# Two hidden pairs of every feed-forward layer multiplied without the seven-product scheme, and the stream sums made earlier

## The chip, the cores and the metric

The kernel runs on one core of one Trainium2 chip. The metric is the device time in microseconds (us) of one execution; a profile of one execution is taken beside it. The engines are named as in the profile: PE is TensorE (matmuls), PEld its weight loads, DVE VectorE, ACT ScalarE, POOL GpSimd, SP SyncE. The last two issue most of the DMAs here.

## What is computed

One step of a trunk of two layers for 512 frames of a prompt and 32 frames of a sample stream, together T = 544 columns, model width 1024, hidden width 2816, all in fp32:

```
for i in range(DEPTH):
    x = x + FFN_RES * swiglu(rms_norm(x, p['ffn1_norm'][i]), ...)
    ...                                   # conv module for i = 0, differential attention for i = 1
    x = x + m
    x = x + FFN_RES * swiglu(rms_norm(x, p['ffn2_norm'][i]), ...)
y = rms_norm(x, p['final_norm'])

def swiglu(h, w_gate, w_up, w_down):
    return (jax.nn.silu(h @ w_gate) * (h @ w_up)) @ w_down
```

So there are four feed-forward layers, called FFN0 to FFN3 here, in the order FFN0, conv mixer, FFN1, FFN2, attention mixer, FFN3, final norm. The caches and states that the mixers return don't bear on the change.

## The kernel before

**Data.** The stream x lies transposed in eight tiles x0 to x7 of 128 channels by 544 columns. A product in fp32 is three matmuls in a rounded format (high x high, high x low, low x high): each operand is split into a high part (`whi`, `xh`, `hh`), made by ACT, and a low part (`wlo`, `xl`, `hl`), made by DVE as the difference. A matmul takes 128 x 128 weights and 272 of the 544 columns.

**A feed-forward layer.** Hidden channels are done in 22 blocks of 128, each with a gate and an up row. Rather than multiply gate and up with both halves of the columns and all eight tiles (2 x 8 x 2 x 3 = 96 matmuls), a block uses a scheme of seven products P1 to P7 over quarters of the matrices (7 x 4 x 3 = 84 matmuls). The scheme needs differences of the stream (`xd`, L395, `quarters`), sums of the stream (`xt`, split to `xth` and `xtl`, L415, `quarter_sums`), and sums of the weights: `ws`, to which POOL adds by an accumulating DMA (`add_stripe`, L268), and `s`, made by DVE (`total`, L606). The normalisation factor r of a column is multiplied in behind the products: squares of x are summed over channels by small matmuls with a matrix of ones (L463), then come a root on ACT, a reciprocal on DVE and a spread to all partitions by two DMAs over DRAM (`norm_c`, L494). FFN0 and FFN2 give each tile's squares to PE (`square`, `add_squares`, L443); FFN1 and FFN3 add them up on DVE in `acc` first (`norm_sq`, L372). The down products (D) are done in groups of blocks (`FCH`, L33), with x updated after each (`evict`, L628).

**Order.** `layer_order` (L152) writes the order of the products (jobs) by hand. `task` puts the work of DVE and ACT at a job's number; on each engine it runs in the order written. FFN0 starts P1 0, P1 1, P2 0, P2 1, P1 2, P2 2, P5 0, ... . FFN1 and FFN2 are one program; there FFN2's first products stand between the last eight down products of FFN1. The stream sums are made after the last x of a layer is known, except for FFN2, where they stand at the down products 4 to 7. Weights come through rings of tiles (`wr`, `ws`, `wd`) by SP's queue; a ring's next load is issued when its oldest tile was used.

**Memory.** PSUM has a pool for the feed-forward layers, with tiles pq (2, of two banks), pd (1, of two banks) and py (2, of one bank), and one for each mixer (tiles a; m and t). A pool is closed before the next one opens, and the next pool's first instruction waits for all tiles of the old one. X's and Z's sums of the scheme share a pq tile, each a bank of it.

## Time and profile before

| what | us |
|---|---|
| median of three runs | 2069.58 |
| lowest and highest of them | 2066.18, 2071.45 |
| the profiled execution | 2068.29 |
| its span in the trace | 2066.5 |
| TensorE busy in it | 1969.7 |
| VectorE busy | 1537.5 |
| ScalarE busy | 1001.9 |

The trace belongs to the profiled execution, which lies between the lowest and the median run. The span runs from the first instruction to the last; the 1.8 us that the execution is longer lie around it. Busy times are sums over instructions: an engine that is busy 95% of the span can still be at its limit in one stage and wait in another, so the stages are looked at one by one below.

### The profile page before, as it was taken

What the parts mean: (1) busy time and instruction counts of PE and PEld (TensorE: products, weight loads), DVE (VectorE), ACT (ScalarE), POOL (GpSimd) and SP (SyncE); (2) the same over time, 40 slices, a digit from 0 to 9 for tenths busy, and PEclk for the clock granted to TensorE, in tenths of its full rate; (3) what the DMA queues carried; (4) which work ended last, traced back from release to release, by engine and by line L of the source; (5) the groups of instructions that cost most, each with busy time, mean ns of one, the idle gap of its engine ahead of it and who ended that gap; (6) DMA issues with size and microseconds to landing.
All of it is one profiled execution on the core that took longest, in us unless ns stands there. A gap on an engine that the chain in (4) does not pass through costs nothing.

```text
span 2066.5 us, 39057 instructions
## 1 busy us (share of the span) xinstructions
PE 1969.7 (95%) x15564; PEld 1923.2 (93%) x15564; DVE 1537.5 (74%) x2748; ACT 1001.9 (48%) x1931; POOL 184.0 (9%) x217
## 2 busy tenths in 40 slices
...
GB/s 190 176 157 147 139 142 94 77 126 171 145 62 196 151 155 143 144 142 156 23 192 153 146 152 139 97 93 84 89 84 89 63 126 192 158 142 145 144 73 74
DMA packets 114405, 267.01 MB, mean 129 GB/s; under 512 B 12040, under 2 KB 27952, under 8 KB 114224
## 3 DMA queue, kind: packets, MB, share of 16 engines
...
q8 instruction: 123, 2.02, 0.4%
...
HBM read 255.16 MB, written 9.31 MB: 128 GB/s over the span
## 4 chain that ended last, share of the span: by engine, by line
PE 80%; DVE 8%; ACT 5%; DMA 4%; issue 1%; SPq 0%; POOL 0%; DVEq 0%; ACTq 0%; POOLq 0%
PE pq L527 34%; PE pd L345 7%; PE pd L351 7%; PE pd L348 7%; PE py L527 5%; DMA ws<-gu 2%; PE a L345 2%; PE a L348 2%; PE a L351 2%; PE m L345 2%; DVE wlo L119 2%; PE m L348 2%; PE m L351 2%; PE a L843 1%; ACT whi L302 1%
## 5 line engine op out<-in xcount | busy, mean ns | idle before, releaser
L527 PE MATMUL pq<-xh,whi 128*128 128x272 f32 x1008 | 296.3, 294 | 27.0 <-ACT whi L1440 7.6
L527 PE MATMUL pq<-xh,wlo 128*128 128x272 f32 x1008 | 294.6, 292 | 2.6 <-DVE wlo L119 2.6
L527 PE MATMUL pq<-xth,whi 128*128 128x272 f32 x1008 | 290.6, 288 | 4.5 <-DVE u L119 4.5
L527 PE MATMUL pq<-xl,whi 128*128 128x272 f32 x1008 | 292.7, 290 | 0.4 <-DVE xl L410 0.2
L527 PE MATMUL pq<-xtl,whi 128*128 128x272 f32 x1008 | 290.0, 288 | 0.0
L527 PE MATMUL pq<-xth,wlo 128*128 128x272 f32 x1008 | 289.3, 287 | 0.0
L119 DVE TENSOR_TENSOR wlo<-wr,whi 128x512 fp32r<-128x512 f32 (+1 forms) x228 | 186.7, 823 | 123.6 <-ACT whi L302 122.6
L345 PE MATMUL pd<-hh,whi 128*128 128x272 f32 x1272 | 264.9, 290 | 3.6 <-DVE x L635 3.6
L348 PE MATMUL pd<-hl,whi 128*128 128x272 f32 x1272 | 262.5, 287 | 0.0
L351 PE MATMUL pd<-hh,wlo 128*128 128x272 f32 x1272 | 262.4, 288 | 0.0
L302 ACT ACTIVATE whi<-wd 128x512 fp32r<-128x512 f32 (+1 forms) x280 | 166.5, 600 | 145.6 <-issue 117.1
L527 PEld LDWEIGHTS pq<-xh,whi 128*128 128x128 f32 x1008 | 192.7, 191 | 32.8 <-ACT whi L1440 8.2
L272 POOL DMA_DIRECT2D ws<-gu x88 | 106.0, 1211 | 1303.5 <-DVE wlo L119 919.3
L119 DVE TENSOR_TENSOR wlo<-wd,whi 128x512 fp32r<-128x512 f32 (+1 forms) x280 | 183.2, 655 | 36.7 <-ACT whi L302 33.0
L345 PEld LDWEIGHTS pd<-hh,whi 128*128 128x128 f32 x1272 | 199.0, 188 | 4.6 <-issue 4.6
L348 PEld LDWEIGHTS pd<-hl,whi 128*128 128x128 f32 x1272 | 200.1, 189 | 0.0
L351 PEld LDWEIGHTS pd<-hh,wlo 128*128 128x128 f32 x1272 | 199.1, 188 | 0.0
L119 DVE TENSOR_TENSOR wlo<-ws,whi 128x512 fp32r<-128x512 f32 x176 | 120.4, 687 | 101.7 <-ACT whi L302 101.6
L527 PEld LDWEIGHTS pq<-xh,wlo 128*128 128x128 f32 x1008 | 192.9, 191 | 3.2 <-DVE wlo L119 3.1
L527 PEld LDWEIGHTS pq<-xth,whi 128*128 128x128 f32 x1008 | 189.6, 188 | 6.4 <-ACT e L569 2.6
L527 PEld LDWEIGHTS pq<-xl,whi 128*128 128x128 f32 x1008 | 192.8, 191 | 0.9 <-DVE xl L410 0.9
L527 PEld LDWEIGHTS pq<-xth,wlo 128*128 128x128 f32 x1008 | 190.0, 188 | 0.0
...
## 6 DMA issues: line engine op xcount, KB each, us to landing
...
wd<-dn SPq DMA_DIRECT2D x128, 256.0 KB, 2.9
...
```

The lines of the kernel that those rows point to most:

```text
L119: nc.vector.tensor_tensor(out=out, in0=in0, in1=in1, op=op)
L272: nc.gpsimd.dma_start(out=c["t"].rearrange("p (a c) -> p a c", a=2), in_=c["add"], accum_op=ALU.add)
L302: nc.scalar.activation(out=hi, in_=src, func=AF.Copy)
L345: nc.tensor.matmul(out=ps[:, s, :HT], lhsT=wh, rhs=xh[:, s * HT:(s + 1) * HT], start=first, stop=False)
L348: nc.tensor.matmul(out=ps[:, s, :HT], lhsT=wh, rhs=xl[:, s * HT:(s + 1) * HT], start=False, stop=False)
L351: nc.tensor.matmul(out=ps[:, s, :HT], lhsT=wl, rhs=xh[:, s * HT:(s + 1) * HT], start=False, stop=last)
L527: nc.tensor.matmul(out=out, lhsT=wt[:, a:a + P], rhs=b, start=first and k == 0 and z == 0, stop=last and k == 3 and z == 2, skip_group_che ...
L843: nc.tensor.matmul(out=o, lhsT=w[:, t * P:(t + 1) * P], rhs=xt[:, q, t:t + NU], start=t == 0, stop=t == NJ - 1)
```

## The change

- Blocks 0 and 1 of each layer (`PLAIN = 2`) are multiplied plainly. Their jobs are Ga, Gb (gate with tiles 0 to 3 and 4 to 7) and Ua, Ub (up), 24 matmuls each; r is multiplied in from PSUM (`by_r`). They stand first in each layer, so the scheme starts with block 2. In FFN2, Ga 0 stands between the down products 5 and 6 of FFN1, the other plain jobs behind the last.
- The stream sums of FFN1 and FFN3 for k = 0 to 2 are made in the mixer's last outputs (o = 4 to 6), the fourth early in the layer. Those of FFN0 and FFN2 are made at jobs around Ga 1. The low half of one set is made where the next set starts. The differences are made behind the plain jobs (`quarter_diff`), over the second half of `xh` and `xl`.
- All layers sum their squares on DVE (`norm_sq`). The weights of the scheme's first blocks are loaded behind the spread of r.
- PSUM: pq becomes four single banks; X and Z have one each. Last down products use pairs of single banks ("qq", "yy") and are evicted in two operations.
- Pools are opened with `reuse_waits="tile"`: the first use of a new tile waits for the old tiles that lay there, not for the whole pool. One pool `ar` of six tiles serves the conv weights, the sums of the stream and attention's splits.
- In the conv mixer and in attention, the norm's matmuls move some steps back; attention's first q step isn't taken before step 14.
- The prologue loads and splits gate and up of block 0 instead of the gates of blocks 0 and 1. `FCH` becomes (2, 4, 4, 4, 4, 4).

The diff, cut to its core:

```diff
-FCH = (3, 4, 4, 4, 3, 4)
+FCH = (2, 4, 4, 4, 4, 4)
 QC = 512
 AHEAD = 4
+PLAIN = 2
...
+        head = "Ga 0 Ua 0 Gb 0 Ub 0 Ga 1 Ua 1 Gb 1 P1 2 Ub 1 P2 2 P1 3 P2 3 P6 2 P6 3 P5 2 P7 2 P7 3 P5 3 P4 2".split()
+        head = list(zip(head[::2], map(int, head[1::2])))
         if f:
-            order += held[:4]
-            for d, (kind, i) in zip(held[4:], (("P1", 0), ("P1", 1), ("P5", 0), ("P5", 1))):
-                go(kind, i)
-                order.append(d)
-            head = "P2 0 P2 1 P1 2 P2 2 P5 2"
-        else:
-            head = "P1 0 P1 1 P2 0 P2 1 P1 2 P2 2 P5 0 P5 1 P5 2"
-        head = (head + " P6 0 P6 1 P6 2 P7 0 P7 1 P4 0 P3 0 P7 2 P4 1 P3 1 P4 2 P1 3 P3 2 P2 3").split()
-        for kind, i in zip(head[::2], head[1::2]):
-            go(kind, int(i))
...
+            order += held[:6]
+            go(*head.pop(0))
+            order += held[6:]
+        for kind, i in head:
+            go(kind, i)
+        down = [("D", f, o, 0) for o in range(KD)]
+        for i in range(PLAIN + 1, KF):
+            first = i == PLAIN + 1
+            if not first:
+                go("P6", i)
+            go("P3", i - 1)
...
+                if kind in ("Ga", "Ua"):
+                    (gate if kind == "Ga" else both)[f, i] = chunk("wr", g[2 * i + (kind == "Ua")], DM, 2)
...
+    def quarter_diff(k, gc):
+
+        todo = nst.pop("diff", None)
         if k < KD // 2:
...
+            d = ffn_pool[0].tile([P, HT], F32, tag="e", name="xd", bufs=8)
+            two(d, x[k][:, :HT], x[k][:, HT:], ALU.subtract)
+            nst["diff"] = (d, xh[k][:, HT:], xl[k][:, HT:], vcol(gc + k))
...
+        if k == 0:
+            nst["t"] = [arena() for _ in range(6)]
+        todo = nst.pop("sum", ())
+        if k < KD // 2:
+            b = tp.tile([P, T], F32, tag="g", name="xg")
+            nc.scalar.activation(out=b, in_=x[k + KD // 2], func=AF.Copy, scale=vcol(gc + k + KD // 2))
+        for src, h, l in todo:
+            nc.scalar.activation(out=h, in_=src, func=AF.Copy)
+        if k < KD // 2:
...
-            nc.vector.scalar_tensor_tensor(out=t4, in0=t[:, HT:], scalar=-1.0, in1=b[:, :HT],
+            nc.vector.scalar_tensor_tensor(out=b[:, :HT], in0=t[:, HT:], scalar=-1.0, in1=b[:, :HT],
...
-        with tc.tile_pool(name="hp", bufs=1) as hp, \
-             tc.tile_pool(name="pf", bufs=1, space=bass.MemoryType.PSUM) as pf:
+        with tc.tile_pool(name="hp", reuse_waits="tile", bufs=1) as hp, \
+             tc.tile_pool(name="pf", reuse_waits="tile", bufs=1, space=bass.MemoryType.PSUM) as pf:
...
+            def by_r(tag, kind):
+
+                if "sum" in nst:
+                    quarter_sums(KD // 2, None)
+                t = b[tag] = tp.tile([P, T], F32, tag=tag, name=tag)
+                ps = st[kind, f, m]
+                if isinstance(ps, list):
+                    for z, p in enumerate(ps):
+                        two(t[:, z * HT:(z + 1) * HT], p[:, :HT], nst["r"][:, z * HT:(z + 1) * HT], ALU.mult)
+                else:
+                    two(halves(t), pv(ps), halves(nst["r"]), ALU.mult)
...
+            if m < PLAIN:
+                g1 = at["Ga", f, 1, c] + (2 if f == 0 and entry else 1)
+                n1 = max(at["Gb", f, m, c] + 1, g1)
+                n2 = max(at["Ub", f, m, c] + 1, g1)
+                task(n1, lambda: by_r("g", "G"))
+                task(n1, silu)
+                task(n2, lambda: by_r("u", "U"))
+                task(n2, prod, True)
+                n3 = n2 + (3 if m else 1)
+                task(n3, hidden)
+                task(n3, hidden_lo, True)
+                return
...
-            nc.vector.scalar_tensor_tensor(out=halves(x[o]), in0=pv(ps), scalar=0.5, in1=halves(x[o]),
-                                           op0=ALU.mult, op1=ALU.add)
+            for out, src in [(x[o][:, z * HT:(z + 1) * HT], p[:, :HT]) for z, p in enumerate(ps)] \
+                    if isinstance(ps, list) else [(halves(x[o]), pv(ps))]:
+                nc.vector.scalar_tensor_tensor(out=out, in0=src, scalar=0.5, in1=out, op0=ALU.mult, op1=ALU.add)
...
+            for ring, n in DEPTH.items():
+                while nload[ring] < n:
+                    load(ring)
...
-        if entry == "start":
-            for k in range(KD):
-                task(2 + k, lambda k=k: square(k))
-        else:
-            task(8, norm)
-        for k in range(KD // 2):
-            task(k, lambda k=k: quarter_sums(k, which[0][0]), True)
+        for f in range(len(which)):
+            g1 = at["Ga", f, 1, 0]
+            start = entry and f == 0
+            task(g1 - (1 if f else 0 if start else 2), norm)
+            gc = which[f][0]
+            sums_at = (-1, 0, 1, 4, 5) if start else (-2, -1, 0, 4, 5) if f else (None, None, None, -3, -2)
+            for k, n in enumerate(sums_at):
+                if n is not None:
+                    task(g1 + n, lambda gc=gc, k=k: quarter_sums(k, gc), True)
+            for k in range(KD // 2 + 1):
+                task(g1 + 3 + k, lambda gc=gc, k=k: quarter_diff(k, gc), True)
...
-                held = j["c"] == len(FCH) - 1 and (i < KD // 2 or f + 1 == len(which))
-                ps = st["d", f, i, j["c"]] = ptile("q" if i % 2 and held or (j["c"], i) == (len(FCH) - 2, KD - 1) else "d")
+                tag = "d"
+                if j["c"] == len(FCH) - 1:
+                    tag = ("d", "qq", "d", "qq", "yy", "d" if f + 1 < len(which) else "qq", "yy", "d")[i]
+                elif (j["c"], i) == (len(FCH) - 2, KD - 1):
+                    tag = "qq"
+                ps = st["d", f, i, j["c"]] = ptile(tag)
                 for k in range(j["n"]):
                     hh, hl = hid[f, j["m0"] + k]
                     mm3(ps, (hi[:, off:], lo[:, off:]), k, hh, hl, k == 0, k == j["n"] - 1)
             else:
-                if kind == "P1":
-                    st["q", f, i] = ptile("d" if i == 2 else "q")
+                if kind in ("Ga", "Ua"):
+                    st[kind[0], f, i] = ptile({("Ga", 1): "yy", ("Ua", 1): "d"}.get((kind, i), "qq"))
+                elif kind == "P1":
+                    st["x", f, i] = ptile("q")
+                elif kind == "P5":
...
+                if kind[0] in "GU":
+                    for k in range(4):
+                        kk = k + 4 * (kind[1] == "b")
+                        mm3(st[kind[0], f, i], (hi[:, off:], lo[:, off:]), k, xh[kk], xl[kk], kk == 0, kk == KD - 1)
+                    u["left"] -= 1
+                    continue
...
             if first:
-                proj(pg, w_get(), range(KD - 2))
-                norm_a(alloc()[:, 0, :], [nst["acc"]], AF.Sigmoid)
-                proj(pg, cur[0], range(KD - 2, KD))
+                proj(pg, w_get())
                 pa = alloc()
                 proj(pa, w_get(), range(1))
+                norm_a(alloc()[:, 0, :], [nst["acc"]], AF.Sigmoid)
+                proj(pa, cur[0], range(1, KD - 2))
                 norm_b(alloc())
...
             norm_sq(o)
+            if o < KD - 1:
+                quarter_sums(o - KD // 2, next_gc)
...
-                at_step(24 * h + 8 * i + 8 + c["f"][i], f, h)
+                at_step(max(24 * h + 8 * i + 8 + c["f"][i], 14), f, h)
...
+                norm_sq(k)
             for c in gates:
                 used(c)
                 used(c)
+            load("ws")
...
         def between(o):
             quarters(o, V_F1 + KD)
-            square(o)
-            if o >= KD // 2:
-                quarter_sums(o - KD // 2, V_F1 + KD)
+            norm_sq(o)
...
-        with tc.tile_pool(name="psa", bufs=4, space=bass.MemoryType.PSUM) as pp:
+        with tc.tile_pool(name="psa", reuse_waits="tile", bufs=4, space=bass.MemoryType.PSUM) as pp:
             conv(psum(4, [P, 2, 512], pp, "a", 4), V_F2)
...
-
-        with tc.tile_pool(name="psb", bufs=2, space=bass.MemoryType.PSUM) as pp:
+            if KD // 2 <= o < KD - 1:
+                quarter_sums(o - KD // 2, V_F2 + KD)
+
+        with tc.tile_pool(name="psb", reuse_waits="tile", bufs=2, space=bass.MemoryType.PSUM) as pp:
             attn(psum(2, [P, 2, 512], pp, "m", 2), psum(4, [P, 512], pp, "t", 4), into_ffn)
```

How the order of instructions moves is shown at three places. Names carry the number of a buffer; a row is line, operation, output <- inputs, shape.

DVE in the conv mixer's tail, before: from the eviction of x6 (L987) past that of x7. `acc` adds a square, `xl` is a low part for FFN1, `wlo` the low part of FFN1's weights, `xt` the first stream sum.

```order
L987 SCALAR_TENSOR_TENSOR x6_93<-a_6820,vecs_72,x6_93 128x544
L410 SCALAR_TENSOR_TENSOR xl5_6814<-x5_92,vecs_72,xh5_6813 128x544
L119 TENSOR_TENSOR acc_6658<-acc_6658,sq_6880 128x544
L119 TENSOR_TENSOR wlo_6885<-wr_6622,whi_6884 128x512
L119 TENSOR_TENSOR wlo_6885<-wr_6698,whi_6884 128x512
L987 SCALAR_TENSOR_TENSOR x7_94<-a_6883,vecs_72,x7_94 128x544
L410 SCALAR_TENSOR_TENSOR xl6_6877<-x6_93,vecs_72,xh6_6876 128x544
L119 TENSOR_TENSOR acc_6658<-acc_6658,sq_6943 128x544
L410 SCALAR_TENSOR_TENSOR xl7_6940<-x7_94,vecs_72,xh7_6939 128x544
L119 TENSOR_TENSOR wlo_6973<-wr_6762,whi_6972 128x512 x2
```

The same place after the change, from the eviction of x6 to that of x7 (L1030); `xt` and the write to `xg` are a set of sums for k = 2, `ar` the low halves of the set for k = 1:

```order
L1030 SCALAR_TENSOR_TENSOR x6_94<-a_6801,vecs_75,x6_94 128x544
L405 SCALAR_TENSOR_TENSOR xl5_6785<-x5_93,vecs_75,xh5_6784 128x544
L123 TENSOR_TENSOR acc_6630<-acc_6630,sq_6861 128x544
L435 SCALAR_TENSOR_TENSOR xt_6868<-x2_90,ngain_87,xg_6864 128x272
L437 SCALAR_TENSOR_TENSOR xt_6868<-x2_90,ngain_87,xt_6868 128x272
L439 SCALAR_TENSOR_TENSOR xg_6864<-xt_6868,xg_6864 128x272
L123 TENSOR_TENSOR ar_6719<-xt_6795,ar_6716 128x544
L123 TENSOR_TENSOR ar_6721<-xg_6791,ar_6718 128x272
L123 TENSOR_TENSOR wlo_6876<-wr_6597,whi_6875 128x512
L123 TENSOR_TENSOR wlo_6876<-wr_6658,whi_6875 128x512
L1030 SCALAR_TENSOR_TENSOR x7_95<-a_6874,vecs_75,x7_95 128x544
```

Between the two evictions stand five operations for the stream sums that stood behind the last eviction before.

DVE at the down products between FFN1 and FFN2, before: from the eviction of x5 (L635) to that of x6, with a set of stream sums in between (`xt`, `xt4`, `xtl`):

```order
L635 SCALAR_TENSOR_TENSOR x5_92<-pd_11496,x5_92 128x544
L410 SCALAR_TENSOR_TENSOR xl5_11531<-x5_92,vecs_72,xh5_11530 128x544
L427 SCALAR_TENSOR_TENSOR xt_11537<-x1_88,ngain_86,xg_11535 128x272
L429 SCALAR_TENSOR_TENSOR xt_11537<-x1_88,ngain_86,xt_11537 128x272
L431 SCALAR_TENSOR_TENSOR xt4_11538<-xt_11537,xg_11535 128x272
L119 TENSOR_TENSOR xtl1_11540<-xt_11537,xth1_11539 128x544
L119 TENSOR_TENSOR xtl1_11540<-xt4_11538,xth1_11539 128x272
L119 TENSOR_TENSOR wlo_11526<-wr_10884,whi_11525 128x512
L119 TENSOR_TENSOR wlo_11593<-wr_11030,whi_11592 128x512
L635 SCALAR_TENSOR_TENSOR x6_93<-pd_11563,x6_93 128x544
```

After, from the eviction of x2 (L658) past that of x3, which comes in two halves:

```order
L658 SCALAR_TENSOR_TENSOR x2_90<-pd_11278,x2_90 128x544
L123 TENSOR_TENSOR acc_11236<-acc_11236,sq_11311 128x544
L405 SCALAR_TENSOR_TENSOR xl2_11309<-x2_90,vecs_75,xh2_11308 128x544
L123 TENSOR_TENSOR wlo_11342<-wd_11130,whi_11341 128x512
L658 SCALAR_TENSOR_TENSOR x3_91<-pq_11314,x3_91 128x272
L658 SCALAR_TENSOR_TENSOR x3_91<-pq_11315,x3_91 128x272
L123 TENSOR_TENSOR acc_11236<-acc_11236,sq_11352 128x544
L405 SCALAR_TENSOR_TENSOR xl3_11350<-x3_91,vecs_75,xh3_11349 128x544
L123 TENSOR_TENSOR wlo_11342<-wr_10848,whi_11341 128x512
```

The sums are gone from here; each tile's square is now added to `acc` on DVE, and the add stands ahead of the tile's low part.

SP's queue at FFN0's start, before, up to the spread of r (`row`, then `r`):

```order
L262 DMA wd_159<-gu0 128x512
L262 DMA wd_161<-gu0 128x512
L262 DMA wd_163<-dn0 128x384
L262 DMA ws_468<-gu0 128x1024
L262 DMA ws_490<-gu0 128x1024
L262 DMA wr_509<-gu0 128x1024
L262 DMA wd_517<-dn0 128x384
L491 DMA row_540<-r4_535 4x136
L492 DMA r_539<-row_540 128x544
```

After:

```order
L268 DMA wr_143<-gu0 128x1024
L1468 DMA vecs_75<-vec 128x317
L268 DMA wr_214<-gu0 128x1024
L268 DMA wr_216<-gu0 128x1024
L268 DMA ws_218<-gu0 128x1024
L479 DMA row_352<-r4_347 4x136
L480 DMA r_351<-row_352 128x544
L268 DMA ws_355<-gu0 128x1024
L268 DMA ws_357<-gu0 128x1024
```

The spread of r has moved ahead of the loads of `ws` for the later blocks and of `wd`, which now follow it.

## Rows read from the trace of the kernel before

**Rows 1.** The page, part 1 (busy us, share of the span, instructions) for TensorE, and part 4, the chain that ended last, by engine.

```profile
PE 1969.7 (95%) x15564; PEld 1923.2 (93%) x15564; DVE 1537.5 (74%) x2748; ACT 1001.9 (48%) x1931; POOL 184.0 (9%) x217
...
PE 80%; DVE 8%; ACT 5%; DMA 4%; issue 1%; SPq 0%; POOL 0%; DVEq 0%; ACTq 0%; POOLq 0%
```

**Rows 2.** Busy time by stretch, the whole program: for each stretch in us from the span's start its length, then busy us and instructions of TensorE, its weight loads, DVE, ACT and POOL, the granted clock of TensorE as a share of 2.4 GHz, the share of the DMA engines, GB/s. The first is the start of FFN0, the second steady work, then the starts of FFN1, FFN2 and FFN3.

```profile
0.00:80.00 80.00, 55.66 (x389) 48.70 (x390) 57.98 (x120) 46.60 (x91) 10.52 (x18) 0.89 0.68 186
80.00:360.00 280.00, 280.00 (x2240) 280.00 (x2239) 208.19 (x366) 133.75 (x261) 18.07 (x15) 1.00 0.52 140
...
620.00:680.00 60.00, 48.33 (x353) 45.92 (x352) 48.29 (x88) 35.25 (x67) 8.47 (x7) 0.94 0.71 184
...
960.00:1065.00 105.00, 93.61 (x738) 87.82 (x737) 80.50 (x144) 58.22 (x109) 6.05 (x5) 0.98 0.42 112
...
1670.00:1728.00 58.00, 47.46 (x345) 45.00 (x345) 46.79 (x86) 34.14 (x65) 8.44 (x7) 0.94 0.70 185
```

**Rows 3.** The waits of TensorE over the whole span: tile and line that waited, who was waited for, us in total, times, longest.

```profile
PE py L463 <- DVE e L119: 8.8, 1, 8.8
PE pq L527 <- ACT whi L1440: 7.6, 3, 5.3
...
PE pq L527 <- ACT whi L302: 6.8, 2, 3.4
...
PE m L345 <- DVE x L635: 3.6, 1, 3.6
PE a L345 <- DVE x L635: 3.6, 1, 3.6
PE pd L345 <- DVE x L635: 3.6, 4, 1.4
```

**Rows 4.** TensorE at FFN0's start and FFN2's: the group of the small squares' matmuls in the stretch 0 to 80 and in 960 to 1065 (busy us, mean ns | idle before), and between them two rows of the timeline (start, us): the last of the first 48 products, and what came next.

```profile
L463 PE MATMUL py<-sq,ones_d 128*32 128x136 f32 x64 | 4.2, 345 | 8.8 <-DVE e L119 8.8
...
19.01 0.29 PE L527 MATMUL py<-xh,wlo 128*128 128x272 f32 x1
28.14 0.68 PE L463 MATMUL py<-sq,ones_d 128*32 128x136 f32 x8 [8.83 <-DVE e L119]
...
L463 PE MATMUL py<-sq,ones_d 128*32 128x136 f32 x64 | 3.6, 298 | 0.0
```

**Rows 5.** DVE at the end of the conv mixer and the start of FFN1, from the timeline (start, us, engine, line, operation, tiles; in brackets its idle time before and who ended it): one output of the mixer up to the next one's eviction (L987), then one set of stream sums and its low halves; the last row is an output of the attention mixer.

```profile
612.24 0.78 DVE L987 SCALAR_TENSOR_TENSOR x<-a,vecs,x 128x544 f32<-128x544 f32 x1
...
614.39 0.72 DVE L119 TENSOR_TENSOR acc<-acc,sq 128x544 f32<-128x544 f32 x1 [0.68 <-ACT sq L378]
...
616.24 0.78 DVE L987 SCALAR_TENSOR_TENSOR x<-a,vecs,x 128x544 f32<-128x544 f32 x1
...
626.57 0.50 DVE L427 SCALAR_TENSOR_TENSOR xt<-x,ngain,xg 128x272 f32<-128x272 f32 x1
...
628.34 1.08 DVE L119 TENSOR_TENSOR xtl<-xt,xth 128x544 fp32r<-128x544 f32 x2 [0.25 <-ACT xth L434]
629.33 0.49 DVE L427 SCALAR_TENSOR_TENSOR xt<-x,ngain,xg 128x272 f32<-128x272 f32 x1
...
1672.42 0.72 DVE L1334 TENSOR_TENSOR x<-m,x 128x544 f32<-128x544 f32 x1 [2.01 <-PE m L351]
```

**Rows 6.** FFN1's last down products before FFN2, from the timeline: the eviction of x4 on DVE, then on ACT the high part and the square of it.

```profile
999.89 0.72 DVE L635 SCALAR_TENSOR_TENSOR x<-pd,x 128x544 f32<-128x544 f32 x1
...
1000.64 0.75 ACT L406 ACTIVATE xh<-x,vecs 128x544 fp32r<-128x544 f32 x1 [1.39 <-DVE x L635]
1001.30 0.64 ACT L445 ACTIVATE sq<-x 128x544 f32<-128x544 f32 x1
```

**Rows 7.** The spread of r, from the timeline: SyncE's DMAs (`SPq`: the row to DRAM, then from there to 128 partitions) and the first use on DVE in FFN0, and the two DMAs in FFN1.

```profile
51.47 0.60 SPq L491 DMA_DIRECT2D row<-r  x1
56.18 0.33 SPq L492 DMA_DIRECT2D r<-row  x1
...
61.67 0.44 DVE L119 TENSOR_TENSOR g<-e,r 128x272 f32<-128x272 f32 x1 [1.33 <-DMA r<-row]
...
647.68 0.52 SPq L491 DMA_DIRECT2D row<-r  x1
649.28 0.33 SPq L492 DMA_DIRECT2D r<-row  x1
```

**Rows 8.** The entry of the conv mixer, from the timeline: the evictions of x5 and x7 (L635) on DVE, then TensorE's last matmul of FFN0 and its first of the mixer.

```profile
401.28 0.72 DVE L635 SCALAR_TENSOR_TENSOR x<-pq,x 128x544 f32<-128x544 f32 x1
...
407.03 0.72 DVE L635 SCALAR_TENSOR_TENSOR x<-pq,x 128x544 f32<-128x544 f32 x1
...
403.84 0.41 PE L351 MATMUL pq<-hh,wlo 128*128 128x272 f32 x2
407.89 0.49 PE L345 MATMUL a<-xh,whi 128*128 128x272 f32 x2 [3.65 <-DVE x L635]
```

**Rows 9.** Busy time by stretch again, short ones around the idle times of TensorE (columns as in rows 2).

```profile
28.75:40.75 12.00, 9.50 (x53) 8.11 (x50) 10.16 (x20) 7.34 (x15) 0.00 (x0) 0.50 0.11 20
...
409.50:412.50 3.00, 3.00 (x16) 3.00 (x15) 1.71 (x2) 1.81 (x2) 0.00 (x0) 0.50 0.15 22
...
1690.50:1695.00 4.50, 4.50 (x21) 4.50 (x21) 2.82 (x6) 2.21 (x5) 0.00 (x0) 0.50 0.02 4
...
1004.00:1022.00 18.00, 12.34 (x106) 10.80 (x105) 13.95 (x25) 10.31 (x20) 0.00 (x0) 1.00 0.04 12
```

215 lines of the change are left out of this document (92 added, 123 removed).

## The prediction

> **What bounds the kernel now.** I read the page's busy shares and its chain first: TensorE (PE) is busy 1969.7 of 2066.5 us and carries 80% of the chain, VectorE (DVE) 8% [rows 1]. So time is won only where PE waits or where it has fewer columns to stream. Next I read busy time stretch by stretch [rows 2]. From 80 to 360 us PE is busy all the time: 2240 matmuls in 280.00 us, 0.125 us for each 128x272 product. I call **loss** of a stretch its length less 0.125 us times its 128x272 matmuls; small norm matmuls (128x136) count as loss. The four starts of a feed-forward layer (FFN0 to FFN3) are then:
> FFN0, 0 to 80: 389 matmuls less 64 small ones [rows 4], 325 x 0.125 = 40.6, loss 39.4.
> FFN1, 620 to 680: 353 less 8 small (its one norm, where the 64 were eight), 345 x 0.125 = 43.1, loss 16.9.
> FFN2, 960 to 1065: 738 less 64 small [rows 4], 674 x 0.125 = 84.2, loss 20.8.
> FFN3, 1670 to 1728: 345 less 8, 337 x 0.125 = 42.1, loss 15.9.
> Together 93.0 us, the stock the change can draw on. The waits of PE [rows 3] say what they are made of: 8.8 us behind `e` at the first squares, 7.6 and 6.8 us for weight halves (`whi`), and, at the entry of either mixer, 3.6 us for the last eviction of x.
>
> **The added matmuls.** A plain block takes 96 products of 128x272 where the seven-product form takes 84. Two blocks in each of four layers: 8 x 12 = 96 more, x 0.125 = **+12.0 us**, all on PE and on the path, since PE has no idle time in the steady part [rows 2].
>
> **FFN0's start.** PE finished its first 48 products at 19.3 us, bound by x and the weight pieces as they came, and then stood from 19.3 to 28.14, because the bank for the squares is freed by `e` on DVE, which stood behind two sets of stream sums there [rows 4]. In the changed order 8 plain half blocks of 24 matmuls stand there, which need x and weights alone. The same arrivals put 72 matmuls (Ga 0, Ua 0, Gb 0) at about 20 us, loss 20 - 9 = 11, and the next 100 run without the sums, to about 32.5. Behind that I expect 0 to 3 us at P1 2, whose bank is freed only when r is there: the reciprocal can be done at about 25 (my estimate: x7's square added by 20.5, then norm, root and reciprocal), and the spread of r over the partitions took 10.2 us from its first transfer's issue to its first use in this stage (51.47 to 61.67) and less elsewhere [rows 7]; I take 2. In SyncE's (SP's) queue fewer weight loads stand ahead of the row than now, and the loads for the weight sums stand behind the spread (the order excerpt), so the second of those sums may be late; that is in the next figure. Between nothing and two sets of sums (5.5 us, worked out in the next part) in the P6 and P5 products, which come quicker than DVE can make sums and weight sums: I take 5, near the upper end, since DVE has the evictions of the plain blocks to do as well. With 3 us of smaller waits and 1 of half clock (both estimates): 11 + 2 + 5 + 3 + 1 = 22. Gain 39.4 - 22 = **17.5** (16 to 19.5).
>
> **FFN1's start.** The stream sums of k = 0 to 2 move into the last three outputs of the conv mixer. There DVE needs 4.0 us for an output (612.24 to 616.24, with 0.68 us of waiting for ACT's square inside), and PE 48 x 0.125 = 6.0. A set of sums is three operations and two lows: 626.57 to 628.34 and 628.34 to 629.33, 2.8 us [rows 5]. So DVE's turn becomes 4.0 + 2.8 = 6.8, or about 6.5 if the wait inside the set is filled: it falls 0.5 to 0.8 us behind for each output and starts from a backlog here. By the end x7's eviction, which now follows PE's last product at once, comes about 3.7 us after it; Ga 0's second matmul waits for that eviction, since its bank lies under the mixer's last accumulator. With 1.5 us of half clock after it and 1 of small waits the loss is about 6. What falls away is the wait for sums and for `whi` behind them. Gain 16.9 - 6 = **10.9** (8 to 13).
>
> **FFN3's start.** The same, but in the attention mixer's tail DVE waits 2.01 us for PE before each output [rows 5], so the added 2.8 leaves it about 0.8 behind for each of three: x7 some 2.4 us late, loss 4.4. Gain **11.5** (9 to 13).
>
> **FFN2's start.** Here the sums leave the down products and the squares leave PE: DVE adds them up instead (64 small matmuls took 3.6 us [rows 4]). But the add waits for ACT, and it is written ahead of the low half: eviction 0.72, of x, then ACT's `xh` and `sq`, which end at 1001.94, 2.05 us after the eviction's start [rows 6], add 0.65, low 0.7, a weight low 0.6: 4.0, with small waits 4.5, against 24 x 0.125 = 3.0 on PE. Over eight outputs the plain Gb 0, which needs x7, ends some 6.3 us later than PE alone would (8 x 1.5 = 12 us of DVE's lag, less about 6 that the plain Ga 0 and the first part of Gb 0 fill); with up to two sets of sums, 5.5 us, waited for at P6, the loss is 6.3 to 11.8 and I take 10.8. Gain **10** (8 to 13). The excerpt of DVE's order shows the new place of the add.
>
> **The mixers' entries.** PE stood from 404.1 to 407.89 until x7 was evicted, since the pool closes as a whole [rows 8]; 3.0 us after that ran at a granted clock of 0.50, 1.2 GHz, with 16 records in place of 24 [rows 9]. With a wait for each tile the first accumulator needs x5's bank alone, evicted at 401.28 [rows 8]; x7's low half is due at k = 7, 42 matmuls or 5.2 us later, when it is there. Gain 3.65 + 1.0, less 0.1: **4.5** (2 to 6). At the attention's entry the same 3.6 us [rows 3] and up to 2 us of half clock, less about 0.8 for the q step that is moved behind: **5** (3 to 6). Removed constants, single banks of their own for X and Z, one conv tile more, and shorter first hidden chunks: nothing, PE's full stretches hide them; if that cover went, the evictions that now come in two pieces would cost at most a second 0.72 [rows 6] each, some 5 in a layer, 14 us in all.
>
> **Sum.** 17.5 + 10.9 + 11.5 + 10 + 4.5 + 5 = 59.4, less 12.0: 47.4 us. From the profiled execution's 2068.3 us (span 2066.5 and 1.8 around it; the median of the runs, 2069.6, is 1.3 above) this gives 2020.9. I predict **2021**. The ends of the terms, 46 and 70.5, less 12, give 2010 to 2034.
>
> **Rivals.**
> 1. *VectorE becomes the bound of the starts.* For: it is the engine the starts wait for already [rows 3], and each added operation is in order behind a wait for ACT [rows 5, 6]. If a down product's turn is 5.5 us instead of 4.5 (8 us), x7 comes 3 us later in FFN1 and FFN3 (6 us), and half clock follows three times at 1.6 (5 us), the time is 2021 + 19 = **2040**. Against: most of the sums now lie beside plain products.
> 2. *r comes late everywhere.* The plain accumulators are held until r. In FFN1 the row's issue and r's were 1.6 us apart (647.68, 649.28), in FFN0 4.7 [rows 7]. With FFN0's 10.2 us in every layer, P1 2 waits 1.5 us in three layers and 3 in FFN0 instead of 2, with a little half clock: **2028**.
> 3. *The waits by tile do nothing at the mixers* (another buffer still holds the first product back): 9.5 back, **2030**.
> 4. *The starts are almost free*: three of them lose 4 us each less than I take, and 2 us of half clock are gone: **2007**. For: the sums are off PE's path in all of them. Against: the down products' 4.5 us a piece before FFN2, which nothing shortens.
> 5. *Slower: half clock through the plain heads.* In the stretch 28.75 to 40.75 PE was busy 9.50 of 12 us and yet ran at 0.50 all along [rows 9]. If the short waits for banks keep it there, a matmul takes 4.5 / 21 = 0.214 instead of 0.125 [rows 9], 2.1 us more for a half of 24; 32 halves cost 69 us, and the time is **2090**. From 22 halves on, two thirds of the heads, the change is slower than before. Against: from 1004 to 1022 PE was busy only 12.34 of 18 us, in pieces with waits of 1.4 us for banks between them, and the granted clock was 1.00, 2.4 GHz [rows 9]; the long slow stretches followed idle times of 3.4 us and more [rows 3, 8, 9], and such ones I expect at one or two places only.
> The Trainium skill speaks for this rival: "TensorE: Matmul & The Clock Gate", section "A second HAM failure mode: psum-queue depth-cycling", reports a kernel in which cycling through PSUM banks left PE idle for short times so often that its clock swung between the two levels. By that rule the time would be rival 5's. The trace agrees with it before 41 us and not from 1004 to 1022.
>
> **How the numbers follow.** About 0.3% (6 us) is what a measurement of this kernel can tell from no change. Forecast (2010 to 2034, likeliest 2021) 0.52; rival 1, 0.18; rival 2, 0.08; rival 3, 0.06; rival 4, 0.08; rival 5, 0.05; the remaining 0.03 for two of the losses together, which would end near no change. Rival 1 may reach 2045 where its lateness grows with each output. The range that leaves out no more than 2 in 10 is **2005 to 2043**: it holds the forecast, rivals 2 to 4 and most of rival 1. Faster by over 0.3%: 0.91; within 0.3%: 0.04; slower: 0.05.
>
> **What would show it.** In the changed profile: no wait of PE near 19 us and none for `e` at squares; at the mixers' entries no 3.6 us wait and a clock of 1.00; a wait of 2 to 4 us for x in FFN1's second matmul, with half clock after it; the down products before FFN2's plain head 4.5 us apart with PE waiting for x; FFN0's first 336 matmuls done at 62 to 65 us; 96 more matmuls in the full stretches at 0.125. Wrong would be: full stretches with waits (then the new banks or the shorter chunks cost something), a granted clock of 0.50 through the plain halves, or starts whose loss stays above 81 of the 93 us, from which the added products eat the gain.

## The result, and the profile after

The changed kernel takes 2019.3 us (median, 2017.7 to 2021.9) where the kernel before takes 2068.7 in the same session: ratio 0.976, 95% interval 0.9745 to 0.9780, faster by 49 us. The prediction was 2021 us, in a range of 2005 to 2043. The profiled execution took 2020.5 us, with a span of 2018.7 against 2066.5. Each kernel's time below is the median of its fast executions; one execution of both_orders took 6031.8 us and is left out.

The page of the changed kernel, busy us (share of the span) and instructions, and the chain that ended last:

```profile
PE 1964.4 (97%) x15548; PEld 1929.4 (96%) x15548; DVE 1513.4 (75%) x2722; ACT 979.2 (49%) x1873; POOL 173.9 (9%) x209
...
PE 61%; DVE 6%; ACT 4%; issue 1%; DMA 1%; POOL 0%; DVEq 0%; ACTq 0%
```

PE is busy 1964.4 us where it was 1969.7 [rows 1], though it has 96 products more: most of the small squares are gone (64 took 3.6 us in FFN2 [rows 4]), and less of it runs at half clock. The chain's shares add up to 73% only, so I read nothing from the fall of PE's from 80%. Busy time by stretch (length, busy us of PE, its weight loads, DVE, ACT and POOL, granted clock, DMA share, GB/s), the starts of FFN0, FFN1, FFN2 and FFN3 and two steady stretches between:

```profile
0.00:80.00 80.00, 67.48 (x466) 64.66 (x467) 62.56 (x126) 47.18 (x89) 8.09 (x17) 0.96 0.66 190
80.00:340.00 260.00, 260.00 (x2079) 259.88 (x2078) 196.52 (x344) 125.49 (x245) 18.55 (x17) 1.00 0.53 142
600.00:660.00 60.00, 57.27 (x457) 56.37 (x456) 44.99 (x84) 32.31 (x62) 6.05 (x5) 1.00 0.61 173
660.00:940.00 280.00, 280.00 (x2239) 279.86 (x2238) 210.60 (x370) 134.20 (x261) 21.44 (x18) 1.00 0.57 151
940.00:1045.00 105.00, 99.14 (x764) 97.63 (x763) 80.26 (x149) 56.56 (x104) 3.57 (x3) 0.97 0.33 93
1630.60:1688.60 58.00, 55.10 (x439) 54.15 (x439) 42.61 (x80) 31.87 (x61) 6.03 (x5) 1.00 0.64 178
```

Worked as in the prediction (length less 0.125 us for each 128x272 product; each start has 8 small ones now), the losses are: FFN0 80 - 458 x 0.125 = 22.75 (39.4 before), FFN1 60 - 449 x 0.125 = 3.9 (16.9), FFN2 105 - 756 x 0.125 = 10.5 (20.8), FFN3 58 - 431 x 0.125 = 4.1 (15.9) [rows 2, 4]. The steady stretches are full, so the new banks and the shorter chunks cost nothing there. The first products of the conv mixer, FFN1, the attention mixer and FFN3 (timeline of PE):

```profile
390.06 0.41 PE L352 MATMUL a<-xh,whi 128*128 128x272 f32 x2
...
602.52 0.29 PE L352 MATMUL pq<-xh,whi 128*128 128x272 f32 x1
...
1351.24 0.41 PE L352 MATMUL m<-xh,whi 128*128 128x272 f32 x2
...
1633.92 0.29 PE L352 MATMUL pq<-xh,whi 128*128 128x272 f32 x1
```

The conv mixer took 212.46 us (214.92 before, 407.89 to 622.81) and attention 282.68 (281.78, 1391.51 to 1673.29). With the 3.65 us of waiting that no longer stand ahead of each, they are 6.1 and 2.75 us shorter; but the lengths before end with a wait of FFN1's and FFN3's first product for x (0.97 and 0.91 us), which lies in the stretches of FFN1 and FFN3 too. Counted once, there, it leaves 5.1 and 1.8 for the mixers. All together:

| term | predicted gain | measured |
|---|---|---|
| FFN0's start | 17.5 | 39.4 - 22.75 = 16.6 |
| FFN1's start | 10.9 | 13.0 |
| FFN3's start | 11.5 | 11.8 |
| FFN2's start | 10 | 10.3 |
| conv mixer's entry | 4.5 | 5.1 |
| attention's entry | 5 | 1.8 |
| added products | -12.0 | -12.0 |
| sum | 47.4 | 46.6 (difference of the spans 47.8; the rest lies outside these stretches) |

What PE still waits for (tile and line that waited, who was waited for, us in total, times, longest):

```profile
PE pq L519 <- ACT e L574: 9.2, 4, 3.3
PE a L451 <- POOL d L908: 5.8, 3, 4.8
PE pq L352 <- ACT whi L1477: 5.2, 1, 5.2
...
PE pq L519 <- DVE g L123: 1.9, 1, 1.9
...
PE pq L352 <- DVE x L1030: 1.6, 1, 1.6
PE pq L352 <- DVE x L1384: 1.5, 1, 1.5
PE pq L355 <- DVE xl L405: 1.5, 1, 1.5
PE pq L352 <- ACT xh L404: 1.3, 2, 0.9
...
PE py L519 <- DVE g L123: 0.9, 1, 0.9
...
PE a L886 <- DMA ar<-wtp: 0.7, 1, 0.7
```

The 8.8 us behind `e` at the first squares and the two 3.6 us at the mixers [rows 3] are gone, and of the waits for `whi` the 5.2 us ahead of the very first product are left. What stands first now is `e` again, at another place: P6 3 is added up in the bank that holds P1 3, and ACT has to copy P1 3 into `e` before; PE waits for that copy in all four layers (3.30, 1.17, 3.30 and 1.40 us). Inside the conv mixer the wait for a weight fell from 3.5 to 0.7 us while that for POOL's `d` rose from 3.0 to 5.8; wt_five below shows that the sixth tile is not the cause.

### The profile page after: what moved, and what is told of

The parts are those of the page before. It is cut to its first block, busy times and chain, and to the rows that moved or that the text cites. A ratio compares the mean times of both kernels' runs of the same rounds, so it can differ in the third digit from the quotient of the medians.

```text
span 2018.7 us, 38721 instructions
## 1 busy us (share of the span) xinstructions
PE 1964.4 (97%) x15548; PEld 1929.4 (96%) x15548; DVE 1513.4 (75%) x2722; ACT 979.2 (49%) x1873; POOL 173.9 (9%) x209
## 3 DMA queue, kind: packets, MB, share of 16 engines
q1 hardware_dynamic: 80528, 204.20, 30.4%
## 4 chain that ended last, share of the span: by engine, by line
PE 61%; DVE 6%; ACT 4%; issue 1%; DMA 1%; POOL 0%; DVEq 0%; ACTq 0%
PE pq L519 26%; PE pd L352 6%; PE pd L358 6%; PE pd L355 6%; PE py L519 4%; PE m L352 2%; PE m L355 2%; PE m L358 2%; DVE wlo L123 1%; ACT e L1161 1%; PE t L1174 1%; PE pq L352 1%; PE pq L355 1%; PE a L355 1%; PE t L1218 1%
## 5 line engine op out<-in xcount | busy, mean ns | idle before, releaser
L519 PE MATMUL pq<-ar,whi 128*128 128x272 f32 x1920 | 370.8, 290 | 9.8 <-ACT e L574 9.2
L519 PEld LDWEIGHTS pq<-ar,whi 128*128 128x128 f32 x1920 | 303.4, 189 | 11.2 <-ACT e L574 10.1
L519 PE MATMUL pq<-xh,whi 128*128 128x272 f32 x960 | 276.3, 288 | 1.9 <-DVE g L123 1.9
L519 PE MATMUL pq<-ar,wlo 128*128 128x272 f32 x960 | 278.1, 290 | 0.0
L519 PE MATMUL pq<-xh,wlo 128*128 128x272 f32 x960 | 277.3, 289 | 0.0
L519 PE MATMUL pq<-xl,whi 128*128 128x272 f32 x960 | 276.1, 288 | 0.0
L519 PEld LDWEIGHTS pq<-ar,wlo 128*128 128x128 f32 x960 | 182.3, 190 | 0.0
L308 ACT ACTIVATE whi<-wr 128x512 fp32r<-128x512 f32 (+1 forms) x244 | 174.0, 718 | 16.9 <-PE pq L355 5.2
L519 PEld LDWEIGHTS pq<-xh,wlo 128*128 128x128 f32 x960 | 181.3, 189 | 0.0
L658 DVE SCALAR_TENSOR_TENSOR x<-pd,x 128x544 f32<-128x544 f32 x168 | 120.9, 720 | 78.0 <-PE pd L358 77.8
```

The lines of the kernel that those rows point to most:

```text
L308: nc.scalar.activation(out=hi, in_=src, func=AF.Copy)
L519: nc.tensor.matmul(out=out, lhsT=wt[:, a:a + P], rhs=b, start=first and k == 0 and z == 0, stop=last and k == 3 and z == 2, skip_group_che ...
L658: nc.vector.scalar_tensor_tensor(out=out, in0=src, scalar=0.5, in1=out, op0=ALU.mult, op1=ALU.add)
```

## The experiments

Twelve kernels ran, each beside the kernel before on its chip. "FFN0 x us" and the like are lengths of a stage in the trace, from its first product to that of the next (FFN3's is counted to the final norm's). The ratios of wt_five, plain3_fix, diff_later, low_first and both_orders lie between 0.9740 and 0.9753, about the lower end of the changed kernel's interval (0.9745 to 0.9780), and their intervals overlap it: their times do not tell them from the changed kernel, and what is said of them is read from stages.

### The mixers' entries

**pool_whole**, the changed kernel without the wait by tile in the mixers' pools:

```diff
-tc.tile_pool(name="psa", reuse_waits="tile", bufs=4, ...
+tc.tile_pool(name="psa", bufs=4, ...
-tc.tile_pool(name="psb", reuse_waits="tile", bufs=2, ...
+tc.tile_pool(name="psb", bufs=2, ...
```

> The changed kernel with one thing undone: the PSUM pools of the two mixers wait for the whole old pool again. Theory (the wait by tile is what freed the mixers' entries): PE's 3.65 us wait for x returns at both entries, with granted clock 0.50 behind it (2.0 us lost in the conv mixer, 1.1 in attention, by the distance between the two traces), so 2019.3 + 7.3 + 3.1 = 2030, less what attention's later waits gave away of it (2.0): about 2028. Rival (the moved norm steps and the new order of evictions freed the entries, the pools did nothing): 2019 to 2021 and no wait at the entries.

2030.4 us, ratio 0.9807 (0.9789 to 0.9826): 9 to 11 us slower than the changed kernel. Two waits for x stood there again, 4.0 us each, and behind them the granted clock fell. In the stages the main parts are 4.0 us at FFN0's end, 2.6 in the conv mixer (215.1 for 212.5) and 4.4 in FFN1 and FFN2 with the wait at their end (753.1 for 748.7):

```profile
396.10:400.00 3.90, 3.90 (x20) 3.90 (x21) 2.65 (x3) 2.13 (x3) 0.00 (x0) 0.59 0.00 0
1364.20:1369.00 4.80, 4.76 (x26) 4.79 (x27) 2.65 (x3) 3.46 (x4) 0.00 (x0) 0.64 0.07 20
```

**before_tile**, the kernel before with that edit alone:

```diff
-tc.tile_pool(name="psa", bufs=4, ...
+tc.tile_pool(name="psa", reuse_waits="tile", bufs=4, ...
-tc.tile_pool(name="psb", bufs=2, ...
+tc.tile_pool(name="psb", reuse_waits="tile", bufs=2, ...
```

> The kernel before with one edit: the two pools of the mixers' accumulators wait by tile. Theory: each entry's wait for x of 3.6 us goes or becomes short, with half clock after it: 2068.65 less 7 to 9, 2060 to 2062 (it was mis-sized if the gain is under 5, and all of the mixers' gain lies here if it is 9). Rival: the accumulators find another late owner of their bank, or the low half of x7 is waited for instead, and nothing moves: 2067 to 2069.

2065.7 us, ratio 0.9981 (0.9971 to 0.9990): 3 us and no more. The theory missed. In the trace the conv mixer with its entry is 3.3 us shorter and attention with its own 1.6 longer, a part of which is the granted clock in attention's tail (see the mixers' entries in the next section). The same edit that is worth some 10 us in the changed kernel is worth 3 here, because PE only gets to the norm's first matmul sooner (PE, at the entries of the conv mixer and of attention):

```profile
410.01 0.44 PE L463 MATMUL a<-acc,ones_d 128*32 128x136 f32 x8 [1.38 <-DVE acc L119]
...
1389.75 0.68 PE L463 MATMUL t<-acc,ones_d 128*32 128x136 f32 x8 [3.54 <-DVE acc L119]
```

That matmul needs the square of x7 added to `acc`. In the kernel before it stands behind 36 products in the conv mixer (4.5 us) and behind 18 in attention (2.25 us); in the changed kernel behind 54 in both (6.75 us), and it waits for nothing:

```profile
397.18 0.44 PE L451 MATMUL a<-acc,ones_d 128*32 128x136 f32 x8
...
1358.34 0.44 PE L451 MATMUL t<-acc,ones_d 128*32 128x136 f32 x8
```

So the gain is read as that of the wait by tile and the moved norm together; no run moved the norm alone.

**wt_five**, the changed kernel with five conv tiles instead of six:

```diff
-        WTB = 6
+        WTB = 5
```

> The changed kernel with 5 conv weight tiles loaded ahead in place of 6. In the changed kernel PE's wait for these weights fell from 3.5 to 0.7 us, and its wait for POOL's d tiles right behind rose from 2.0 to 4.8. Theory (POOL's d tiles set the end of that stretch, so an earlier weight only lengthens the next wait): the two waits go back to 3.5 and 2.0, the time stays at 2019 within 1.5. Rival (the sixth tile brings 2.8 us): 2022.

2017.1 us, ratio 0.9740 (0.9722 to 0.9759); the conv mixer took 212.07 us against 212.46. The sixth tile is worth nothing, as forecast, but not for the reason forecast: with five tiles PE's wait for the weight was 0.9 us and not 3.5 again, and that for POOL 6.1 in one piece. What shortened the wait for the weight is open.

### The sums in the mixers

**sums_home**, the stream sums of FFN1 and FFN3 made around Ga 1, as in FFN2:

```diff
-sums_at = (-1, 0, 1, 4, 5) if start else (-2, -1, 0, 4, 5) if f else (None, None, None, -3, -2)
+sums_at = (-1, 0, 1, 4, 5) if start else (-2, -1, 0, 4, 5) if True else ()
...
-            if o < KD - 1:
-                quarter_sums(o - KD // 2, next_gc)
...
-            if KD // 2 <= o < KD - 1:
-                quarter_sums(o - KD // 2, V_F2 + KD)
```

> The changed kernel with the stream sums of the third and fourth feed-forward starts (FFN1, FFN3) made around the second plain gate block, as in FFN2, and no longer in the last outputs of the two mixers. Theory: in the changed kernel the sums in the mixers cost two waits for x7 (1.56 and 1.50 us) and buy short waits of the squares for e (1.17 and 1.40 us against FFN2's 3.30). Put back, the x7 waits go (3.1 us less), the e waits grow to 3.3 us with about 1.5 us of half clock each (7 us more): 2019.3 + 4 = 2023. If the mixers' share of the sums is worth nothing, only the x7 waits go: 2016. Before's 16.9 us of loss at FFN1 would not come back in either case, since the plain halves stand there.

2024.9 us, ratio 0.9788 (0.9772 to 0.9805), some 5 us slower. The waits for x7 fell to 0.75 and 0.69 us, those for `e` rose to 2.28 and 2.92, and the clock fell behind each (here FFN1's and FFN3's):

```profile
640.50:642.00 1.50, 1.50 (x9) 1.50 (x9) 1.50 (x4) 1.50 (x5) 0.00 (x0) 0.53 0.02 5
...
1671.40:1674.00 2.60, 2.59 (x11) 2.60 (x12) 2.60 (x7) 2.21 (x5) 0.00 (x0) 0.50 0.00 0
```

As the theory had it: of the starts' gain, the mixers' share in the sums is a small part.

### How many plain blocks

**plain1**, one plain block (the first chunks as before; the order of the head, the banks and the places of evictions and differences set to match):

```diff
-PLAIN = 2
+PLAIN = 1
...
-        head = "Ga 0 Ua 0 Gb 0 Ub 0 Ga 1 Ua 1 Gb 1 P1 2 Ub 1 P2 2 P1 3 P2 3 P6 2 P6 3 P5 2 ..."
+        head = "Ga 0 Ua 0 Gb 0 Ub 0 P1 1 P2 1 P1 2 P2 2 P5 1 P5 2 P6 1 P6 2 P7 1 P7 2 P4 1"
...
-                g1 = at["Ga", f, 1, c] + (2 if f == 0 and entry else 1)
+                g1 = at["P2", f, 2, c] + 1
```

> The changed kernel with one plain block at each start instead of two, 48 products fewer (6.0 us less). Theory: the plain blocks are the cover under which ACT and DVE make the sums, r and the weight sums; with half of the cover the seven-product form begins 6 us sooner and waits for these at each start, 4 to 8 us each with half clock: 2019 - 6 + 16 to 32 = 2029 to 2045. Rival: one block is cover enough, the waits at the squares stay as they are, and the time is 2013.

2058.4 us, ratio 0.9943 (0.9928 to 0.9958), beyond the forecast 2045. Nearly the whole gain is gone. The products of the scheme came to a bank that is freed by the plain block's eviction, and stood (21.6, 4.8, 6.8 and 4.2 us at the four starts):

```profile
PE pq L519 <- DVE g L123: 37.4, 4, 21.6
```

In FFN0 that was not a wait for r, whose DMA was issued at 24.7 us and for which DVE never stood. The eviction, which is written behind P2 2 here (`g1`), stood in DVE's queue behind low halves of the weight sums, for whose loads ACT, and DVE behind it, waited, and behind sums of the stream (DVE):

```profile
33.63 0.69 DVE L123 TENSOR_TENSOR wlo<-ws,whi 128x512 fp32r<-128x512 f32 x1 [8.34 <-ACT whi L308]
...
40.77 0.69 DVE L123 TENSOR_TENSOR wlo<-ws,whi 128x512 fp32r<-128x512 f32 x1 [3.04 <-ACT whi L308]
...
48.85 0.78 DVE L123 TENSOR_TENSOR g<-pq,r 128x272 f32<-128x272 f32 x2
```

So the run shows what one block is worth in this order. One block with its evictions written ahead of that work was not tried.

**plain3**, three plain blocks:

```diff
-PLAIN = 2
+PLAIN = 3
...
-        head = "Ga 0 Ua 0 Gb 0 Ub 0 Ga 1 Ua 1 Gb 1 P1 2 Ub 1 P2 2 P1 3 P2 3 P6 2 P6 3 P5 2 ..."
+        head = "Ga 0 Ua 0 Gb 0 Ub 0 Ga 1 Ua 1 Gb 1 Ub 1 Ga 2 Gb 2 P1 3 Ua 2 Ub 2 P2 3 P1 4 P2 4 P6 3 P6 4 P5 3 ..."
...
-                task(g1 + 3 + k, lambda gc=gc, k=k: quarter_diff(k, gc), True)
+                task(g1 + 5 + k, lambda gc=gc, k=k: quarter_diff(k, gc), True)
```

> The changed kernel with three plain blocks at each layer's start instead of two (first hidden chunks of 3 and 3). It adds 4 x 12 = 48 products, 6.0 us. Theory: the stalls that are left at the squares (3.3, 1.2, 3.3, 1.4 us, and about 1.5 us of half clock behind each 3.3) are work of DVE and ACT that comes late, and another 12 us of plain products per layer covers it: up to 12 us less, 2014 to 2019. Rival: the stalls come with the work itself, since a square's bank is freed by operations in ACT's queue that stand there behind the same differences, wherever it starts: 2025.

2045.3 us, ratio 0.9885. This tells nothing of the theory: the differences are written over half of `xh` and `xl`, and here that came before the third up block had read them, which therefore multiplied other values and waited for them. **plain3_fix** puts that right (`g1 + 7 + k`):

> As plain3 (three plain blocks at each start, 48 more products, 6.0 us), but with the differences of x begun two steps later still, behind the last plain block that reads what they overwrite. (In plain3 the third plain up block read x's high and low halves after the differences had been written over a part of them, so it multiplied other values and waited for them, 1.4 to 6.5 us at each start.) Theory as for plain3: the waits for e that are left (3.3, 1.2, 3.3, 1.4 us, with about 1.5 us of half clock behind each 3.3) are covered by the third pair, 6.0 us more products against up to 12 us of stalls, 2013 to 2019. Rival: the differences stand in the same place against the squares as before, so the waits for e move along with them unchanged, and the time is 2025.

2019.2 us, ratio 0.9753 (0.9737 to 0.9768), the same as with two blocks and the upper end of the forecast. All waits for `e` at the squares were gone, FFN3's stage took 374.0 us against 372.9, FFN0's 386.8 against 384.9: a third block saves about what it costs. In FFN0 a wait of 3.9 us for a weight and one of 2.1 for an eviction (`u`) stood where the one for `e` had been.

### The waits that were left

**diff_later** (the differences one step later) and **low_first** (before FFN2 the low half of x ahead of the add of its square), each alone and then both:

```diff
-                task(g1 + 3 + k, lambda gc=gc, k=k: quarter_diff(k, gc), True)
+                task(g1 + 4 + k, lambda gc=gc, k=k: quarter_diff(k, gc), True)
```

```diff
             quarters(o, V_F1 + KD)
+            flush()
             norm_sq(o)
```

> The changed kernel with the four stream differences placed one job later, so that on ACT the eviction e of the second X bank stands ahead of one more of their high parts. In the changed kernel PE waits for that e in P6 3: 3.3 us in FFN0 and FFN2, 1.2 and 1.4 in FFN1 and FFN3, with half clock behind the longer ones. Theory (DVE is the bound there, busy 13.3 of the 14 us; ACT only passes its lateness on, and P5 2 needs all differences soon after): e comes 1.5 to 2.5 us earlier, but PE then waits at P5 2; the half clock (1.5 us, twice) goes: 2015 to 2018. Rival (it is ACT's order alone): all four waits and the half clock go, 9.2 + 3, about 2007. A second rival (the differences become late): 2020 to 2024.

> The changed kernel with the low half of x ahead of the add of its square at the down products before FFN2. There DVE's turn is 4.1 us, 1.36 of it idle for ACT's square. Theory (that idle time makes the plain head wait 0.87 and 1.49 us for x7): the turn falls to 3.4 us and both waits go, 2.4 us, while the norm is about 0.7 later: 2017. Rival (DVE's later work in FFN2 is the bound, so PE waits longer at P6 3): 2019 to 2020.

> The changed kernel with two moves of order: the differences of x one step later (as in diff_later, whose FFN0 and FFN2 waits for e fell to 2.1 and 1.2 us) and, before FFN2, the low half of x ahead of the add of its square (as in low_first, where the waits of 0.87 and 1.49 us in the first plain blocks of FFN2 were gone and FFN1 and FFN2 together took 744.9 instead of 748.7 us). Theory: the two moves touch different waits and add up, FFN1 and FFN2 together take about 743 to 744.5 us, the time is 2013 to 2016. Rival: the differences, now later, run into the low halves of weights or of the squares, which wait 1.0 us each, and eat the gain: 2017 to 2019.

diff_later took 2018.9 us (ratio 0.9748, 0.9728 to 0.9767), just above its theory's 2015 to 2018: the waits for `e` fell from 9.2 to 4.0 us in all, and 5.4 us of waits for the differences' own low halves took their place. FFN1 and FFN2 together took 748.2 us, as before (748.7). low_first took 2018.0 (0.9743, 0.9726 to 0.9760); there FFN1 and FFN2 took 744.9: the waits of 0.87 and 1.49 us in Gb 0 and some small ones were gone. both_orders took 2015.9 (0.9751, 0.9729 to 0.9772), with 745.1 for FFN1 and FFN2: low_first's gain again and nothing from diff_later. In the stages that is the rival's account, with 2.7 us of waits for the differences' low halves; the time lies in the theory's range, but its interval holds the rival's too. low_first's 3.8 us can't be read from its time: by the medians it is 1.3 us faster than the changed kernel, by the ratios 3.9. In its profile FFN0, which it leaves alone, was longer: that stage took 388.5 us, in the profiles of the changed kernel, sums_home and wt_five 384.9, 385.0 and 385.9. (The 391.1 in the expectation of wd_low is pool_whole's 391.0, which holds the wait at the mixer's entry.)

What swings there is the wait at P2 2, counted under `py` behind `g`: 0.9 us in the changed kernel, 5.7 in low_first, 6.5 in wt_five (where the wait for `e` behind it was the shorter for it). On its face it is a wait for r. The rows of DVE and ACT in the changed kernel, then ACT's in wt_five, say otherwise:

```profile
33.84 0.43 DVE L123 TENSOR_TENSOR ar<-xg,ar 128x272 fp32r<-128x272 f32 x1
34.19 0.78 DVE L123 TENSOR_TENSOR g<-pq,r 128x272 f32<-128x272 f32 x2
...
40.11 0.69 DVE L123 TENSOR_TENSOR wlo<-wr,whi 128x512 fp32r<-128x512 f32 x1 [4.44 <-ACT whi L308]
40.72 0.72 DVE L123 TENSOR_TENSOR g<-g,u 128x544 f32<-128x544 f32 x1
41.36 0.78 DVE L123 TENSOR_TENSOR g<-py,r 128x272 f32<-128x272 f32 x2
```

```profile
39.45 0.63 ACT L308 ACTIVATE whi<-wr 128x512 fp32r<-128x512 f32 x1 [3.72 <-DMA wr<-gu]
```

```profile
41.92 0.63 ACT L308 ACTIVATE whi<-wr 128x512 fp32r<-128x512 f32 x1 [7.81 <-DMA wr<-gu]
```

The eviction that PE waited for stood in DVE's queue behind a weight's low half, and that behind a load that had not landed. SyncE had issued five loads of the ring `wd` ahead of it. **wd_low** moves these behind it, in FFN0 alone, and keeps low_first:

```diff
-            for ring, n in DEPTH.items():
-                while nload[ring] < n:
-                    load(ring)
+            while nload["ws"] < DEPTH["ws"]:
+                load("ws")
+        def wd_first():
+            while nload["wd"] < DEPTH["wd"]:
+                load("wd")
...
+            if start:
+                task(g1 + 2, wd_first)
```

> The changed kernel with low_first's move (before FFN2 the low half of x ahead of the add of its square) and, in FFN0 alone, SyncE's five first loads of the wd ring issued behind the two weight loads (wr) that they stood ahead of. In the traces so far PE waits 0.9 to 6.5 us at the second product of the third pair (P2 2) for the eviction of the second plain block, which is counted under r (py behind g); but DVE stood there behind a weight's low half, and that behind ACT's high half, which waited 3.72 to 7.81 us for wr to land. Theory: the wait is for that weight, behind 1.3 MB of wd in the queue, and not for r: the wr loads are issued some 2 us sooner and land 4 to 8 us sooner, the wait at P2 2 is under 1 us, FFN0 takes 381 to 384 us (384.9 to 391.1 in the changed kernel and four of its variants), FFN1 and FFN2 together 744 to 745.5; the time is 2012 to 2015. Rival: r itself comes late, or the memory's rate is the limit whatever the order; then FFN0 stays at 385 to 391 and the time is 2016 to 2018.

2013.1 us, ratio 0.9721 (0.9704 to 0.9737). The load was issued at 27.6 us instead of 33.0, ACT had it at 35.9, the wait at P2 2 was gone, and FFN0 took 383.0 us: the weight and not r. The first wait for `e` was untouched (3.30 us). Its cause, in ACT's order in the changed kernel:

```profile
51.76 0.52 ACT L418 ACTIVATE xh<-xd,vecs 128x272 fp32r<-128x272 f32 x1 [2.02 <-DVE xd L123]
52.19 0.38 ACT L574 ACTIVATE e<-pq 128x272 f32<-128x272 f32 x1
```

This copy is that of P1 3, written behind P1 3 (`task(a["P1"] + 1, ...)`), whose last product started at 44.88 us; it stands behind a difference for which ACT waits for DVE. **wd_low_early** begins the differences two steps sooner instead of later, at the first step at which nothing reads any more what they overwrite:

```diff
-                task(g1 + 3 + k, lambda gc=gc, k=k: quarter_diff(k, gc), True)
+                task(g1 + 1 + k, lambda gc=gc, k=k: quarter_diff(k, gc), True)
```

> wd_low with the differences of x begun two steps sooner (right behind the last plain product that reads what they overwrite). In wd_low's trace the squares of P6 still wait 3.30, 1.37, 3.30 and 1.37 us for e at the four starts; in FFN0 ACT's copy into e at 49.20 stood behind a difference's high half that waited 2.02 us for DVE's subtraction at 48.31, which DVE reached only behind a set of sums. Theory: those waits come from the place of the differences in ACT's and DVE's queues; with all four subtractions ahead of that set e comes about 2 us sooner, the waits fall to about 1 us in FFN0 and FFN2 and below 1 in FFN1 and FFN3, and the half clock behind the two long ones (about 1.5 us each) goes: 2013 - 2 x 2.3 - 2 x 1.5 - 1 = 2005 (2003 to 2009). Rival: DVE has the same work ahead of e in whatever order, so something else, the evictions of the plain blocks above all, comes late instead: 2012 to 2015.

2007.4 us, ratio 0.9694 (0.9681 to 0.9707), faster than both kernels. FFN0 took 379.2 us, FFN1 and FFN2 741.2. The waits for `e`, and the first 80 us with no half clock:

```profile
PE pq L519 <- ACT e L574: 1.5, 2, 0.8
```

```profile
0.00:80.00 80.00, 69.06 (x511) 65.43 (x512) 68.13 (x135) 49.97 (x95) 9.24 (x17) 1.00 0.72 200
```

## Why the prediction was right, step by step

**The stock and the bound** held: the steady stretches stayed full at 0.125 us a product, so the 96 added products cost their 12.0 us. Read from the other side: plain1 has 48 products fewer than the changed kernel and, in its order, loses 39 us. What is not shown is how the starts' 51.7 us divide among the plain blocks and the edits that came with them (squares on DVE, single banks, the order of the loads): no run has one without the others. That the sum came within 2 us is in part luck: the terms were off by -0.9, +2.1, +0.3, +0.3, +0.6 and -3.2 us, which nearly cancel.

**FFN0** (gain 17.5, in full 39.4 - 22 = 17.4; was 16.6). The first 75 products were done at 20.0 us, as forecast, the 166th at 32.5 (forecast 172nd). The 2 us at P1 2 came (1.86), but not from r: DVE reached that eviction without a pause, straight from two sets of sums (rows of 33.84 and 34.19 above). What came late at P2 2 was a weight as loaded (wr), not the second weight sum that the prediction had in mind. The 5 us at P6 and P5 were 3.3 us at P6 3. The half clock, put at 1 us, was more: 36 products in 6.22 us at 34.7 to 41.0 and 15 in 3.38 at 52.6 to 56.0 are 1.7 and 1.5 us over 0.125 each. The sum held because errors of either sign met.

**FFN1 and FFN3** (10.9 and 11.5, were 13.0 and 11.8). The mechanism was right, x7's eviction was the wait at the second product, and the size was off: 1.56 us, not 3.7, in FFN1, and 1.50, not 2.4, in FFN3. The step that failed is "starts from a backlog" and a turn of 6.5 to 6.8 us. DVE's evictions in the conv mixer's tail:

```profile
585.07 0.78 DVE L1030 SCALAR_TENSOR_TENSOR x<-a,vecs,x 128x544 f32<-128x544 f32 x1
...
590.71 0.78 DVE L1030 SCALAR_TENSOR_TENSOR x<-a,vecs,x 128x544 f32<-128x544 f32 x1 [0.20 <-PE a L358]
...
597.12 0.78 DVE L1030 SCALAR_TENSOR_TENSOR x<-a,vecs,x 128x544 f32<-128x544 f32 x1
...
603.53 0.78 DVE L1030 SCALAR_TENSOR_TENSOR x<-a,vecs,x 128x544 f32<-128x544 f32 x1
```

The first turn was 5.64 us, since a set's lows are made only with the next set, as the change has it, where the forecast charged every output with a whole set; DVE caught up and waited for PE. The other two were 6.41 against PE's 6.0: 0.8 us late in all, and the eviction itself. In attention the last three turns were 5.97, 6.41 and 6.35 us. Nor did a clock of 0.50 follow (1.5 us in the sum):

```profile
602.50:612.00 9.50, 7.94 (x67) 7.36 (x66) 8.10 (x14) 6.26 (x10) 1.10 (x1) 1.00 0.78 290
1633.90:1642.00 8.10, 6.60 (x58) 6.19 (x56) 7.36 (x13) 5.24 (x8) 0.00 (x0) 1.00 0.78 283
```

**FFN2** (10, was 10.3), right in sum and not in its parts. A down product's turn on DVE was 4.0 to 4.1 us, not 4.5, with the wait for ACT's square as foreseen (DVE, two evictions and the add between):

```profile
960.54 0.72 DVE L658 SCALAR_TENSOR_TENSOR x<-pd,x 128x544 f32<-128x544 f32 x1
962.62 0.73 DVE L123 TENSOR_TENSOR acc<-acc,sq 128x544 f32<-128x544 f32 x1 [1.36 <-ACT sq L385]
...
964.57 0.78 DVE L658 SCALAR_TENSOR_TENSOR x<-pq,x 128x272 f32<-128x272 f32 x2
```

So Gb 0 waited 0.87 and 1.49 us, not 6.3. The 3.3 us for `e` and the half clock behind it made up most of the rest; the forecast had 4.5 there. The add ahead of the low half was the cause of the two waits in Gb 0, as low_first shows.

**The mixers' entries** (4.5 and 5, were 5.1 and 1.8). The waits of 3.65 us went in both; in the conv mixer the half clock behind it, put at 1.0, was worth 1.4 (products 15.15 us from the entry before are at 13.79 now). The prediction gave this gain to the wait by tile; before_tile shows that alone it brings 3 us in both together. It left attention's moved step as a cost of 0.8 us, where the norm moved behind 54 products is a part of what makes the gain. Attention gives 3 us back at its other end. PE's waits inside it are 8.7 us in all against 8.1 before, but twice in its tail the granted clock fell, with no wait above 1.4 us ahead of it. The rows are the changed kernel's two stretches, then the same place in the kernel before and in diff_later:

```profile
1578.10:1581.50 3.40, 3.40 (x17) 3.40 (x16) 2.01 (x7) 2.19 (x4) 0.00 (x0) 0.50 0.00 0
1595.20:1598.60 3.40, 3.40 (x15) 3.40 (x16) 1.48 (x3) 1.29 (x2) 0.00 (x0) 0.50 0.00 0
...
1613.00:1640.00 27.00, 23.21 (x178) 20.41 (x177) 16.19 (x45) 14.26 (x31) 0.00 (x0) 1.00 0.06 20
...
1565.00:1600.00 35.00, 31.14 (x240) 27.94 (x239) 21.67 (x49) 18.40 (x40) 0.54 (x1) 1.00 0.14 46
```

The variants that keep attention's entry show the same: 279.3 to 279.7 us where the clock stayed up in the tail (diff_later, plain3, plain3_fix), 280.6 to 281.1 with one such stretch (wt_five, low_first, plain1), 281.8 to 282.7 with two (the changed kernel and the rest). At 279.3 the gain would be 5.2, as forecast. What decides whether the clock falls there is not shown.

**The rivals.** Rival 1 (DVE the bound, 2040) fell with turns of 4.1 and 6.4 us. Rival 2 (r late) fell, though r did come late: in FFN1 and FFN3 the spread took 11.4 us from the row's issue (612.40 and 1643.75) to r's first use, more than FFN0's 10.2 before, and DVE stood for it; but PE had plain products all that time and waited for no eviction there (DVE):

```profile
623.75 0.79 DVE L123 TENSOR_TENSOR g<-pq,r 128x272 f32<-128x272 f32 x2 [5.49 <-DMA r<-row]
```

Rival 3 fell with pool_whole. Rival 4's 2007 was not reached by the changed kernel, but wd_low_early reached it by three moves of order. Rival 5 fell: in the plain halves of FFN1 and FFN3, which change banks all the time, the granted clock was 1.00, 2.4 GHz. The swing that the Trainium skill reports for such cycling ("TensorE: Matmul & The Clock Gate", "A second HAM failure mode: psum-queue depth-cycling") is not in these rows.

## What to carry to other kernels

A cheaper scheme with a long preparation can start later at no loss if plain work fills the time. Measure how much cover the preparation needs, in the order in which it runs: half of it gave nearly nothing in the one order tried (2058 us), and half as much again paid only for itself (2019). A wait that a profile puts down to one operand is followed back through the queues of the engines that make it: two of the waits here were not for r and not for the squares, but for what stood ahead in DVE's and ACT's queues, and another order of a few instructions and loads gave 12 us (2019.3 to 2007.4). And an edit that takes one wait away is worth what the next wait in line allows: waiting by tile brought 3 us in one kernel and some 10 in the other.

## What the runs showed of the chip

- The order of loads in one queue set when a weight was there: issued at 30.4 us, behind five loads of the ring `wd`, it was used at 41.9 (wt_five); issued at 27.6, ahead of them, at 35.9 (wd_low). The place in the queue is not all: in the changed kernel it was issued at 33.0, behind them too, and used at 39.5. There the DMA engines moved 360 GB/s at a busy share of 1.06 from 34.7 to 41 us.
- A wait alone did not tell whether the clock would fall: behind waits of 1.56 and 1.50 us it stayed at 1.00; behind 2.28 us in sums_home it was 0.53 from 1.3 us on; behind 3.30 us it was 0.53 for 3.4 us in FFN0 (52.6 to 56.0) and 0.50 in FFN2 (1013.0 to 1015.6); but behind 2.22 us at 33.66 in wd_low_early it was 1.00. In attention's tail it fell with no wait above 1.4 us, in some profiles twice, in some once, in some not at all.
